# A decoder layer on one core: one seven-product k-pair less in the first key pair and one more in three up pairs, splits asked for earlier, and the last k-pair's order reversed

## The chip, the cores and the metric

The kernel runs on one core of a Trainium2 chip. The metric is the device time of one execution in microseconds, of which the median over several runs is taken. Three runs of the kernel before gave 1991.73 us as their median (1990.47 to 1993.38).

## The reference

One layer of a decoder on 256 tokens of width 2048, in float32: a retention mixer and a gated linear recurrence in parallel, merged by sigmoid gates; cross-attention to 256 memory tokens; a gated feed-forward part with a causal convolution; a final RMS norm.

```python
def memory_cross_attention(hn, mem_n, w_q, w_k, w_v, w_o):
    q = (hn @ w_q).reshape(b, s, XA_HEADS, XA_HEAD_DIM)
    k = (mem_n @ w_k).reshape(b, m, XA_HEADS, XA_HEAD_DIM)
    v = (mem_n @ w_v).reshape(b, m, XA_HEADS, XA_HEAD_DIM)
    logits = jnp.einsum("bshd,bmhd->bhsm", q, k).astype(jnp.float32) * (XA_HEAD_DIM ** -0.5)
    p = jax.nn.softmax(logits, axis=-1).astype(v.dtype)
    return jnp.einsum("bhsm,bmhd->bshd", p, v).reshape(b, s, D_MODEL) @ w_o

def conv_gated_ffn(hn, w_up, conv_w, conv_b, w_down):
    up = causal_dwconv(hn @ w_up, conv_w, conv_b)
    gate, val = jnp.split(up, 2, axis=-1)
    return (jax.nn.silu(gate) * val) @ w_down

# in the layer
hn = rmsnorm(h, norm_mix_w[l])
q, k, v, g_ret, xr, yr, g_a, g_b = jnp.split(hn @ w_in[l], offsets, axis=-1)
...
h = h + merged @ w_mix_out[l]
mem_n = rmsnorm(mem, norm_mem_w[l])
h = h + memory_cross_attention(rmsnorm(h, norm_xa_w[l]), mem_n, xa_w_q[l], xa_w_k[l], xa_w_v[l], xa_w_o[l])
h = h + conv_gated_ffn(rmsnorm(h, norm_ffn_w[l]), ffn_w_up[l], ffn_conv_w[l], ffn_conv_b[l], ffn_w_down[l])
return rmsnorm(h, final_norm_w)
```

The widths: 2048 for the model, 5632 for the feed-forward part, 4 attention heads of 512.

## The kernel before

**Products.** Every matmul takes a 128x128 block of tokens as the stationary operand and 128x512 weights as the moving one, in a reduced-precision float format. To keep float32 accuracy each operand is split in two, a high part (a cast, `hi` on ACT, L350) and a low part (the rest, `lo` on DVE, L351), and a product is three matmuls: high by high, low by high, high by low. The tokens' splits are called `s` (L613 and L614 for a load that is scaled on the way), the weights' ones `hi` and `lo`.

**Pairs and k-pairs.** Most weight matrices are worked through in *pairs*: two blocks of 512 columns at once, for both halves of the 256 tokens. The depth of 2048 is cut into 8 *k-pairs* of two 128-rows each; a k-pair's weights come as one 1 MB load (`raw`, three buffers). `steps_pair` (L476) runs one pair. A plain k-pair is 2 token halves x 2 column halves x 2 rows x 3 = 24 matmuls. Some k-pairs are done in *seven products* instead of eight, as in Strassen's scheme with sums of blocks on both sides: 7 x 3 = 21 matmuls. For that the weights' four sums are formed in place on DVE (L371) by `seven_parts`, which makes seven blocks and so 3 splits of 1024 columns and one of 512 where a plain k-pair has two of 1024; and the tokens' sums `ts` are formed by `sums_of` (L443: `g` L449, three `tq` L455 to L457, a high part on ACT L459, a low part on DVE L460). A token sum is kept and used again by later pairs on the same tokens. Which k-pairs are done so is a tuple in the plan: `SEVEN` = (2, 5), `SEVEN_O` = (3, 5), `SEVEN_U` = (4,), `SEVEN_V` = (5,).

**Accumulators.** `p2` and `p4` (left column block, two token halves) lie in one of three slots of the `acc` pool, `x3` and `n` (right column block) are the two buffers of the `sm` pool, which attention's and retention's small products use too. The seven's other four (`p1`, `p6`, `p7`, `x5`) take two more `acc` slots and are drained after the last seven (L515 to L522) into `o1` and `o2`, the left and the right block. At the pair's end four adds (L532) bring `p2`, `p4`, `x3` and `n` in.

**Order.** TensorE's matmuls run in program order. The other engines' instructions are put in order at build time by a list scheduler that works by priorities; `tc.high_priority` moves some ahead. The weights' splits are asked for two loads ahead (`AHEAD`, L391). `later(n, fn)` puts work n + 1 chunks of weights behind. SP issues all loads and the DMA transposes, in one order. A block of results is turned from rows to columns by `by_dma` (L546): copies to planes on ACT (L554), two DMA transposes (L555), a copy back on ACT (L567, `f`), and then what uses it.

**Around the key pair.** `Pairs` (L663) holds a list of token splits that are made when they are asked for: `ms[k]` loads the memory's columns (`in_mem_t`) and splits them. The first four are asked for during the mixer's last product (L1056), the others by `t = st[k2]` in `steps_pair`, at the k-pair itself. Sums are asked for up to three k-pairs ahead, but for lists only where the element is there already (L496). The order of products is: mixer output, key pair 0, query pair 0, query pair 2, attention of heads 0 and 1, key pair 2, value pair, attention of heads 2 and 3, two value blocks, output.

**Feed-forward part.** 11 up pairs (a gate block and its value block) in parts of 4, 4 and 3. The down product of a part, two pairs over the part's hidden values, stands behind the first up pair of the next; the last down product is done in single blocks. Each up pair's blocks are turned; the convolution (L1166, L1168: `fg`, `fv`) and the gating (L1178, L1179, L591) run during the next product.

Of the kernel before, what the change touches and what calls it, by code (L numbers as in the profile page):

```python
# [26 lines left out]
FF = 5632  # L27
NF = FF // P
BW = 512
KC = 4  # L30
KH = 2
# [10 lines left out]
SEVEN = (2, 5)  # L42
SEVEN_O = (3, 5)
SEVEN_U = (4,)
SEVEN_V = (5,)

O_Q, O_K, O_V, O_G = 0, 1024, 2048, 4096
# [22 lines left out]
def both(w, c, seven=SEVEN, row=0, nk=NT, apart=BW):  # L70

    return w, row, nk, (c, c + apart, seven)


def weight_plan():

    plan = []
    for g in range(2):
        keys = [("w_in", 0, NT, c + g * BW) for c in (O_Q, O_K)]
        values = [("w_in", 0, NT, O_V + b * BW) for b in range(2)]  # L80
        plan += keys + [both("w_in", O_V + 1024, SEVEN_V)] if g else [keys[0], values[0], keys[1], values[1]]
        plan.append(both("w_in", O_G + g * 1024))
    for b in range(4):
        plan += [("w_in", 0, NT, c + b * BW) for c in (O_XR, O_YR)]
    plan += [("w_in", 0, NT, O_GB + b * BW) for b in range(2)] + [both("w_proj_rnn", 0)]
    plan += [both("w_in", O_GB + 1024), both("w_proj_rnn", 1024)]
    plan += [both(w, c + b * BW) for w, c in (("w_in", O_GA), ("w_proj_ret", 0)) for b in (0, 2)]
    plan += [("w_mix_out", 0, NT, b * BW) for b in range(4)]
    plan += [both(w, b * BW) for w, b in (("xa_w_k", 0), ("xa_w_q", 0), ("xa_w_q", 2), ("xa_w_k", 2))]
    plan += [both("xa_w_v", 0)] + [("xa_w_v", 0, NT, b * BW) for b in (2, 3)]  # L90
    plan += [both("xa_w_o", 0, SEVEN_O)] + [("xa_w_o", 0, NT, b * BW) for b in (2, 3)]
    for kind, *a in ff_plan():
        if kind == "down" and sum(a) < NF // 4:
            plan += [both("ffn_w_down", b * BW, SEVEN, a[0] * BW, 4 * a[1]) for b in (0, 2)]
        elif kind == "down":
            plan += [("ffn_w_down", a[0] * BW, 4 * a[1], b * BW) for b in range(4)]
        else:
            plan.append(both("ffn_w_up", a[0] * BW, SEVEN_U, apart=FF))
    return plan


def gate_up_at():

    return [w for w, *_ in weight_plan()].index("ffn_w_up")


def ff_plan():

    out, b0 = [], 0
    for nb_ in FF_PARTS:  # L110
        ups = [("up", b) for b in range(b0, b0 + nb_)]
        if b0:
            ups[1:1] = [("down",) + before]
        out += ups
        before = (b0, nb_)
        b0 += nb_
    return out + [("down",) + before]
# [48 lines left out]
def hybrid_layer(  # L166
# [34 lines left out]
    def big(shape, dt=F32, s="b"):  # L201
        return bp.tile(shape, dt, tag="big", name=nm(s))

    def tmp(s="t"):
        return tp.tile([P, 2, S], F32, tag="tmp", name=nm(s))

    def acc():
        return pm.tile([P, 2, BW], F32, tag="acc", name=nm("acc"))

    def small(shape=(P, 2, S)):  # L210
        return px.tile(list(shape), F32, tag="sm", name=nm("sm"))
# [39 lines left out]
    def mm(*a, **k):  # L251
        tc.keep_in_program_order(pe.matmul(*a, **k))  # L252


    plan = weight_plan()
    stream = weight_stream()
    ahead, taken, gemms = [], [0], [0]
# [180 lines left out]
    def gemm_n(*args):  # L438
        return ended(steps_n(*args))
# [3 lines left out]
    def sums_of(t, src=None, scale=None):  # L443

        if id(t) in token_sums:
            return token_sums[id(t)][1]
        if src is None:
            src = big([P, 2, S], s="g")
            dve.tensor_tensor(  # L449
                out=src, in0=t[:, :, 0:S].bitcast(F32), in1=t[:, :, S:BW].bitcast(F32), op=ALU.add  # L450
            )
        o = big([P, 2, 4, P], F32R, s="ts")
        s = tmp("tq").rearrange("p a (b n) -> p (a b) n", b=2)
        a = src.rearrange("p j (i n) -> p (j i) n", i=2)
        dve.tensor_tensor(out=s[:, 0:2], in0=a[:, 0:2], in1=a[:, 1::2], op=ALU.subtract)  # L455
        dve.tensor_tensor(out=s[:, 2], in0=s[:, 1], in1=a[:, 0], op=ALU.subtract)
        dve.tensor_tensor(out=s[:, 3], in0=a[:, 2], in1=s[:, 2], op=ALU.add)  # L457
        if scale is None:
            act.copy(o[:, 0], s)  # L459
            dve.tensor_tensor(out=o[:, 1], in0=s, in1=o[:, 0].bitcast(F32), op=ALU.subtract)  # L460
        else:
            act.mul(o[:, 0], s, scale)
            dve.scalar_tensor_tensor(
                out=o[:, 1], in0=s, scalar=scale, in1=o[:, 0].bitcast(F32), op0=ALU.mult, op1=ALU.subtract
            )
        token_sums[id(t)] = (t, o)
        return o
# [8 lines left out]
    def steps_pair(w, row, st, nk, c1, c2):  # L476

        seven = plan[gemms[0]][3][2]
        last = max(seven)
        banks, begun = {}, set()  # L480
        banks["p2"], banks["p4"] = (lambda a: (a[:, 0, :], a[:, 1, :]))(acc())
        banks["x3"], banks["n"] = (small((P, BW)) for _ in range(2))

        def rows_of(name, left, right, end):

            o = banks[name]
            for i, (a, b) in enumerate(((0, 0), (1, 0), (0, 1))):
                mm(o, left[a], right[b], start=name not in begun, stop=end and i == 2, skip_group_check=True)
                begun.add(name)

        o1 = o2 = None
        for k0, n, parts in chunks(nk, w, row, (c1, c2, seven)):
            k2 = k0 // KH
            for i in seven:
                if k2 < i <= k2 + 3 and (not isinstance(st, list) or i < len(st)):
                    sums_of(st[i])  # L496
            t = st[k2]
            own = [
                [(t[:, j, i * P : (i + 1) * P], t[:, j, S + i * P : S + (i + 1) * P]) for j in range(2)]
                for i in range(2)  # L500
            ]
            if k2 in seven:
                if "p1" not in banks:
                    for a, b in (("p1", "p6"), ("p7", "x5")):
                        two = acc()
                        banks[a], banks[b] = two[:, 0, :], two[:, 1, :]
                ts = sums_of(t)
                s3, s1, s2, s4 = ((ts[:, 0, i, :], ts[:, 1, i, :]) for i in range(4))
                lefts = (own[0][0], s4, own[0][1], s1, s3, s2, own[1][1])
                for name, l, r in zip(("p1", "x3", "p2", "x5", "p7", "p6", "p4"), lefts, parts):  # L510
                    rows_of(name, l, r, k2 == last and name in ("p1", "x5", "p7", "p6"))
                if k2 == last:
                    o1, o2 = (big([P, 2, BW], s="o") for _ in range(2))
                    with tc.high_priority(FREE):
                        act.copy(o1[:, 0, :], banks["p1"])  # L515
                        for o, a, b, op in (
                            (o2[:, 0, :], o1[:, 0, :], banks["p6"], ALU.add),
                            (o1[:, 1, :], o2[:, 0, :], banks["p7"], ALU.add),
                            (o2[:, 1, :], banks["x5"], o1[:, 1, :], ALU.subtract),
                            (o2[:, 0, :], banks["x5"], o2[:, 0, :], ALU.subtract),  # L520
                        ):
                            dve.tensor_tensor(out=o, in0=a, in1=b, op=op)  # L522
            else:
                end = k0 + n == nk
                for b, names in enumerate((("p2", "p4"), ("x3", "n"))):
                    for tt, name in enumerate(names):
                        for j in range(KH):
                            rows_of(name, own[tt][j], parts[b * KH + j], end and j == KH - 1)
            yield o1, o2
        with tc.high_priority(FREE):  # L530
            for o, a in ((o1[:, 0, :], "p2"), (o1[:, 1, :], "p4"), (o2[:, 0, :], "x3"), (o2[:, 1, :], "n")):
                dve.tensor_tensor(out=o, in0=o, in1=banks[a], op=ALU.add)  # L532

    def pair(*args):
        return ended(steps_pair(*args))
# [279 lines left out]
    for g in range(2):  # L815
        dec = big([P, 4, S], s="dec")
        vs, turned = [], ([], [])
        for b, o in enumerate((O_Q, O_K)):
# [5 lines left out]
            a = gemm_n("w_in", 0, xs, NT, o + g * BW) if g + b else q0  # L824
# [516 lines left out]
```

## Time and profile before

| | us |
|---|---|
| median of three runs | 1991.73 (1990.47 to 1993.38) |
| profiled execution | 1992.14 |
| its span, first to last instruction | 1990.0 |
| ACT busy | 1392.4 (70%) |
| DMA queues' busy share, mean of 16 engines | 64.3% |

The profile comes from one execution. The page lists, for each engine, its busy time and its count of instructions; groups of instructions carry the line of the program that made them, here often a helper's (L252 for every matmul). A wait such as `PE sm L252 <- DVE o L532` reads: TensorE's matmul into `sm` stood still until DVE's instruction of L532 was done; behind it stand the total time, the number of waits and the longest. In a timeline a row has its start, its duration, the instruction, how often it ran in a row, and in brackets the idle time of the engine before it and what ended it. Matmuls overlap, so a single one shows 0.39 us though the next one starts earlier than that.

### The profile page before, as it was taken

How to read it: one execution, taken by the hardware profiler on the slowest of the kernel's cores; microseconds unless marked ns; L12 is line 12 of the kernel's file. 1: busy time of each engine (PE TensorE's matmuls, PEld its weight loads, DVE VectorE, ACT ScalarE, POOL GpSimd, SP SyncE). 2: the span in 40 equal slices, each digit the busy share in tenths (PEclk: the TensorE clock that was granted, in tenths of full speed). 3: DMA queues.
4: the chain of work that ended last, by engine and by line, in shares of the span. 5: the costliest groups of instructions: out<-in, count | busy, mean ns of one | idle time of the engine just before them, and what ended most of it. 6: DMA issues, size and time to landing. Idle time of an engine off the chain costs nothing.

```text
span 1990.0 us, 24148 instructions
## 1 busy us (share of the span) xinstructions
PE 1966.6 (99%) x8804; PEld 1628.2 (82%) x8804; DVE 1632.3 (82%) x2164; ACT 1392.4 (70%) x1710; POOL 26.1 (1%) x25
## 2 busy tenths in 40 slices
PE   9999999999999999998999999999999999999998
PEld 8888788888888888886888888888888888888887
DVE  6887986899898888767988767778889878899686
ACT  7666658989654656595868677778776577774683
POOL 0000011000000000000000000000000000000000
PEclk9999999999999999998999999999999999999999
DMA  8756567665554556996666666666666567666673
GB/s 332 236 212 181 198 231 204 201 221 192 214 209 169 210 193 200 318 294 201 217 206 201 214 219 221 204 216 218 220 214 211 212 198 224 212 212 234 209 243 117
DMA packets 198343, 429.82 MB, mean 216 GB/s; under 512 B 142160, under 2 KB 146768, under 8 KB 153168
## 3 DMA queue, kind: packets, MB, share of 16 engines
q1 hardware_dynamic: 198224, 428.28, 64.3%
q8 instruction: 69, 1.13, 0.2%
q14 instruction: 50, 0.41, 0.1%
HBM read 390.49 MB, written 4.19 MB: 198 GB/s over the span
## 4 chain that ended last, share of the span: by engine, by line
PE 37%; DVE 8%; ACT 4%; DMA 2%; issue 2%; POOL 0%; POOLq 0%; DVEq 0%; ACTq 0%; SPq 0%
PE acc L252 23%; PE sm L252 14%; DVE lo L351 3%; ACT hi L350 1%; DMA raw<-in_wall 1%; DMA pt<-pl 1%; ACT f L567 1%; ACT pl L554 1%; DVE fg L1168 1%; DVE raw L371 1%; DVE fv L1168 1%; DVE o L522 1%; ACT o L1282 0%; DVE s L591 0%; DVE fo L1179 0%
## 5 line engine op out<-in xcount | busy, mean ns | idle before, releaser
L351 DVE TENSOR_TENSOR lo<-raw,hi 128x1024 fp32r<-128x1024 f32 (+1 forms) x814 | 951.3, 1195 | 275.2 <-ACT hi L350 270.3
L252 PE MATMUL acc<-hi,s 128*128 128x512 f32 (+1 forms) x3636 | 1116.8, 389 | 3.9 <-DVE s L614 2.2
L350 ACT CAST hi<-raw 128x1024 fp32r<-128x1024 f32 (+1 forms) x814 | 804.8, 1021 | 410.2 <-PE acc L252 109.2
L252 PEld LDWEIGHTS acc<-hi,s 128*128 128x128 f32 x3636 | 680.8, 188 | 145.0 <-DVE s L614 4.3
L252 PE MATMUL acc<-lo,s 128*128 128x512 f32 (+1 forms) x1818 | 705.8, 388 | 2.0 <-DVE lo L351 1.9
L252 PE MATMUL sm<-hi,s 128*128 128x512 f32 x1584 | 488.7, 390 | 1.9 <-DVE o L532 1.9
L252 PEld LDWEIGHTS acc<-lo,s 128*128 128x128 f32 x1818 | 341.9, 188 | 73.4 <-DVE lo L351 3.2
L252 PEld LDWEIGHTS sm<-hi,s 128*128 128x128 f32 x1584 | 297.8, 188 | 64.7 <-ACT v L602 2.0
L252 PE MATMUL sm<-lo,s 128*128 128x512 f32 x792 | 308.5, 390 | 0.0
L567 ACT COPY f<-pt 128x1024 uint16<-128x1024 uint16 x128 | 166.8, 1354 | 15.2 <-DMA pt<-pl 14.9
L252 PEld LDWEIGHTS sm<-lo,s 128*128 128x128 f32 x792 | 148.9, 188 | 31.0
L371 DVE TENSOR_TENSOR raw<-raw 128x512 f32<-128x512 f32 x200 | 138.1, 691 | 3.1
L252 PE MATMUL acc<-hi,ts 128*128 128x512 f32 x300 | 92.9, 391 | 0.0
L554 ACT COPY pl<-o 128x1024 uint16<-128x1024 uint16 x68 | 67.6, 1040 | 6.7 <-DVE o L1002 6.7
L252 PEld LDWEIGHTS acc<-hi,ts 128*128 128x128 f32 x300 | 56.6, 189 | 11.9
L252 PE MATMUL acc<-lo,ts 128*128 128x512 f32 x150 | 59.0, 393 | 0.9 <-DVE lo L351 0.8
L554 ACT COPY pl<-rows 128x1024 uint16<-128x1024 uint16 x40 | 39.8, 1044 | 20.6 <-DVE rows L578 10.6
L532 DVE TENSOR_TENSOR o<-o,acc 128x512 f32<-128x512 f32 x62 | 39.9, 689 | 7.3 <-PE acc L252 7.3
L522 DVE TENSOR_TENSOR o<-o,acc 128x512 f32<-128x512 f32 x62 | 42.6, 687 | 0.1
L532 DVE TENSOR_TENSOR o<-o,sm 128x512 f32<-128x512 f32 x62 | 40.9, 689 | 0.1
L522 DVE TENSOR_TENSOR o<-acc,o 128x512 f32<-128x512 f32 x62 | 40.0, 690 | 0.4
L1168 DVE SCALAR_TENSOR_TENSOR fv<-f,pf,fv 128x255 f32<-128x255 f32 (+1 forms) x88 | 38.7, 486 | 0.0
(191 smaller groups left out, 1054.9 us busy)
## 6 DMA issues: line engine op xcount, KB each, us to landing
raw<-in_wall SPq DMA_DIRECT2D x352, 1024.0 KB, 4.8
nat<-in_x SPq DMA_DIRECT2D x8, 512.0 KB, 9.3
raw<-in_wall SPq DMA_DIRECT2D x7, 512.0 KB, 5.8
pt<-pl SPq DMA_TRANSPOSE x128, 3.3
nat<-in_mem SPq DMA_DIRECT2D x4, 512.0 KB, 9.1
home<-nat SPq DMA_DIRECT2D x4, 512.0 KB, 6.6
nat<-home SPq DMA_DIRECT2D x4, 512.0 KB, 7.2
xt<-in_x_t SPq DMA_DIRECT2D x3, 512.0 KB, 9.1
```

What stands on the lines that cost most here:

```text
L252: tc.keep_in_program_order(pe.matmul(*a, **k))
L350: act.copy(hi[:, cs], src[:, cs])
L351: dve.tensor_tensor(out=lo[:, cs], in0=src[:, cs], in1=hi[:, cs].bitcast(F32), op=ALU.subtract)
L371: dve.tensor_tensor(out=o, in0=a, in1=b, op=ALU.add)
L522: dve.tensor_tensor(out=o, in0=a, in1=b, op=op)
L532: dve.tensor_tensor(out=o, in0=o, in1=banks[a], op=ALU.add)
L554: act.copy(planes[:, tt], words[:, tt])
L567: act.copy(halves_[:, :, :, cs], turned_[:, :, :, cs])
L1168: dve.scalar_tensor_tensor(out=y[:, s:S], in0=z[:, j, 0 : S - s], scalar=pf[:, 2 - s, t : t + 1], in1=y[:, s:S], op0=ALU.mult, op1=ALU.add,)
```

## The change

Four edits.

- The first key pair (`xa_w_k`, block 0) is planned with `SEVEN_V` in place of `SEVEN`: k-pair 5 in seven products and no longer k-pair 2. In the same line the blocks' columns are written as 2 * BW; the pairs are the same.
- In `steps_pair`, where the tokens are a `Pairs`, the splits of two k-pairs ahead are asked for, behind the test for the sums and ahead of `t = st[k2]`.
- An up pair gets `MORE_U` = (2, 4) in place of `SEVEN_U` = (4,) where the plan's entry ahead of it is not an up pair. These are the first up pair of the first part and the second of the other two, because in these the down product stands between the first and the second.
- In the last k-pair of each pair the right block (`x3`, `n`, with the second half of the weights) comes ahead of the left one (`p2`, `p4`), and the four adds at the end follow this order.

```diff
+MORE_U = (2, 4)
...
-    plan += [both(w, b * BW) for w, b in (("xa_w_k", 0), ("xa_w_q", 0), ("xa_w_q", 2), ("xa_w_k", 2))]
+    plan += [both("xa_w_k", 0, SEVEN_V), both("xa_w_q", 0), both("xa_w_q", 2 * BW), both("xa_w_k", 2 * BW)]
...
-            plan.append(both("ffn_w_up", a[0] * BW, SEVEN_U, apart=FF))
+            plan.append(both("ffn_w_up", a[0] * BW, MORE_U if plan[-1][0] != "ffn_w_up" else SEVEN_U, apart=FF))
...
             for i in seven:
                 if k2 < i <= k2 + 3 and (not isinstance(st, list) or i < len(st)):
                     sums_of(st[i])
+            if isinstance(st, Pairs):
+                st[min(nk // KH - 1, k2 + 2)]
             t = st[k2]
...
                 end = k0 + n == nk
-                for b, names in enumerate((("p2", "p4"), ("x3", "n"))):
+                blocks = list(enumerate((("p2", "p4"), ("x3", "n"))))
+                for b, names in reversed(blocks) if end else blocks:
                     for tt, name in enumerate(names):
...
         with tc.high_priority(FREE):
-            for o, a in ((o1[:, 0, :], "p2"), (o1[:, 1, :], "p4"), (o2[:, 0, :], "x3"), (o2[:, 1, :], "n")):
+            for o, a in ((o2[:, 0, :], "x3"), (o2[:, 1, :], "n"), (o1[:, 0, :], "p2"), (o1[:, 1, :], "p4")):
                 dve.tensor_tensor(out=o, in0=o, in1=banks[a], op=ALU.add)
```

## The prediction

> **What bounds the kernel now.** I read the page's first part, then the waits of TensorE, then the same stretch for each pair of column blocks, and last the timelines around the few places where TensorE stands still.
>
> ```profile
> span 1990.0 us, 24148 instructions
> PE 1966.6 (99%) x8804; PEld 1628.2 (82%) x8804; DVE 1632.3 (82%) x2164; ACT 1392.4 (70%) x1710; POOL 26.1 (1%) x25
> ```
>
> TensorE is busy 99% of the span. So only two things can move the end: fewer matmuls, or fewer of the 1990.0 - 1966.6 = 23.4 us in which it idles (and of the time in which it is busy at a slow clock). The waits say where those are:
>
> ```profile
> PE sm L252 <- ACT ts L459: 3.8, 2, 3.2
> PE sm L252 <- DVE o L532: 3.2, 4, 1.7
> PE acc L252 <- DVE lo L351: 2.7, 4, 1.0
> PE acc L252 <- DVE s L614: 2.2, 2, 1.7
> PE acc L252 <- ACT s L613: 1.4, 1, 1.4
> ```
>
> The change touches the first two, the fourth and the fifth. Next, stretches from the first matmul of one pair to the first of the next: the first key pair, the query pair behind it, two up pairs that the change extends, one late up pair, and the two down pairs that follow an up pair.
>
> ```profile
> 893.11:950.66 57.55, 49.12 (x187) 37.55 (x186) 44.11 (x64) 33.79 (x47) 0.72 (x1) 0.91 0.61 192
> 950.66:992.83 42.17, 42.17 (x188) 34.91 (x187) 38.97 (x51) 33.94 (x39) 0.00 (x0) 1.00 0.66 225
> 1273.41:1316.25 42.84, 42.84 (x190) 35.47 (x189) 33.26 (x42) 27.85 (x35) 0.70 (x1) 1.00 0.66 223
> 1573.96:1616.80 42.84, 42.84 (x191) 35.47 (x189) 31.27 (x34) 20.50 (x22) 0.00 (x0) 1.00 0.59 209
> 1488.46:1531.80 43.34, 42.50 (x188) 34.83 (x186) 40.43 (x59) 36.35 (x45) 0.00 (x0) 1.00 0.69 213
> 1745.56:1789.06 43.50, 42.45 (x187) 34.84 (x186) 40.29 (x59) 36.51 (x45) 0.00 (x0) 1.00 0.72 212
> ```
>
> Columns: stretch, its length, busy time of PE, PEld, DVE, ACT, POOL, granted clock, DMA share, GB/s. The key pair and the query pair have the same products: six k-pairs of 24 matmuls and two of 21, 186 in all. The query pair does them without a gap: 42.17 / 186 = 0.2267 us for one. The key pair needs 57.55, so 15.4 us are lost in this one place, at a granted clock of 0.91. Its timeline shows them:
>
> ```profile
> 905.42 0.50 PE L252 MATMUL sm<-hi,ts 128*128 128x512 f32 x1 [0.60 <-ACT ts L459]
> 906.51 0.50 PE L252 MATMUL sm<-hi,ts 128*128 128x512 f32 x1 [0.59 <-DVE ts L460]
> ...
> 926.24 0.51 PE L252 MATMUL sm<-hi,ts 128*128 128x512 f32 x1 [3.25 <-ACT ts L459]
> ...
> 927.98 1.05 PE L252 MATMUL acc<-hi,s 128*128 128x512 f32 x2
> ...
> 931.74 0.62 PE L252 MATMUL acc<-hi,s 128*128 128x512 f32 x2
> ...
> 934.00 0.51 PE L252 MATMUL acc<-hi,s 128*128 128x512 f32 x1 [1.41 <-ACT s L613]
> 936.15 0.50 PE L252 MATMUL acc<-hi,s 128*128 128x512 f32 x1 [1.65 <-DVE s L614]
> ...
> 937.74 0.80 PE L252 MATMUL acc<-hi,s 128*128 128x512 f32 x1 [0.58 <-DVE s L614]
> ...
> 938.76 1.05 PE L252 MATMUL acc<-hi,s 128*128 128x512 f32 x2
> ...
> 943.46 0.54 PE L252 MATMUL sm<-lo,s 128*128 128x512 f32 x1
> ```
>
> In brackets stands the idle time and what ended it. Token sums (ts) of k-pairs 2 and 5 come late, then the splits (s) of k-pair 6. Behind the long wait and behind the last ones two matmuls take 1.05 where at 931.74 they take 0.62: the clock is halved, the second time from about 938.3 to 943.5, which costs half of these 5.2 us, 2.6.
>
> **The change part by part.** *First key pair, one seven instead of two.* K-pair 2 becomes plain: +3 matmuls, 3 x 0.2267 = +0.68 us. Its token sums, four weight sums and two of its splits disappear (6 us of DVE work, at the prices below), and the waits at 905.42 and 906.51 with them, for plain products need no ts.
>
> *Splits two k-pairs ahead.* The splits of k-pairs 4 to 7 are asked at 2 to 5, so those of 6 and 7 now stand in front of the weight splits of their own k-pairs; the waits at 934.00, 936.15 and 937.74 go. The sums of k-pair 5 are asked one k-pair earlier than before, no more: the test on the list's length stands ahead of the line that lengthens it. Can they still be late? These rows price the chain:
>
> ```profile
> 905.28 1.34 ACT L567 COPY f<-pt 128x1024 uint16<-128x1024 uint16 x1
> 909.58 1.72 ACT L613 ACTIVATE s<-f,pb 128x256 fp32r<-128x256 f32 x4
> 915.32 0.69 DVE L371 TENSOR_TENSOR raw<-raw 128x512 f32<-128x512 f32 x1
> 920.44 2.37 DVE L351 TENSOR_TENSOR lo<-raw,hi 128x1024 fp32r<-128x1024 f32 x2
> 923.44 0.42 DVE L455 TENSOR_TENSOR tq<-g 128x256 f32<-128x256 f32 x1
> 925.24 0.29 DVE L457 TENSOR_TENSOR tq<-g,tq 128x128 f32<-128x128 f32 x1
> ```
>
> Rows overlap by some 0.1 us, so I use 1.25 for f, 0.6 for 512 elements, 0.4 for 256, 1.14 for a low part, 0.95 for a high part (estimates from these rows and the spacing of their neighbours). In the changed order ACT does, from 905.28: two f, one high part, four s, one high part, two s, one high part: 2.5 + 0.95 + 1.6 + 0.95 + 0.8 + 0.95 = 7.8, to 913.1. DVE then does: low part, s, weight sum, half low part, weight sum, s, weight sum, g, weight sum, low part, three tq, low part, ts: 1.14 + 0.4 + 0.6 + 0.6 + 0.6 + 0.4 + 0.6 + 0.6 + 0.6 + 1.14 + 0.9 + 1.14 + 0.6 = 9.3, to 922.4. TensorE reaches k-pair 5 at 893.11 + 120 x 0.2267 = 920.3 and wants the low ts after four matmuls, at 921.2. So 1.2 us are missing if f starts as it did; it started then behind a ts that is gone, and could start up to 1.6 us earlier, with which nothing is missing. Between 0 and 1.2 I take 0.7. [...] The pair: 42.17 + 0.68 + 0.7 = 43.55, which is **-14.0 us**. On the DMA queue the memory load of k-pairs 4 and 5 moves ahead of one weight load; one issue takes 0.43 us (next row), and the weight load it delays is wanted two k-pairs, 10.9 us, later: nothing.
>
> ```profile
> 909.18 0.43 SPq L223 DMA_DIRECT2D xt<-in_mem_t  x1
> ```
>
> [...]
>
> *A second seven in the first up pair of each part.* "First" is the one whose forerunner in the plan is not an up pair: the 1st, 6th and 10th, for in the later parts the down product stands behind one up pair. 3 x 3 matmuls less: 9 x 0.2267 = **-2.04 us**. Each adds on DVE four weight sums (0.6), one low part of 1024 (1.14) and one of 512 (0.6): 4.1 us; the first also builds the sums of k-pair 2 (g, three tq, ts: 0.6 + 0.9 + 0.6 = 2.1). DVE then has 33.26 + 6.2 = 39.5 of 42.2 in the first, 31.27 + 4.1 = 35.4 in the sixth. ACT's extra 1.5 to 2.1 us find 27.85 and 20.50 busy. Room in both; in the first it is thin, 0 to +1 us. I take 0.
>
> *Last k-pair reversed.* The two `sm` accumulators (x3, n) end 12 matmuls, 2.7 us, earlier and are added first; `acc` (p2, p4) ends last. What waited for the drained `sm` banks:
>
> ```profile
> 233.50 0.70 PE L252 MATMUL sm<-hi,s 128*128 128x512 f32 x2 [1.66 <-DVE o L532]
> 1035.54 0.63 PE L252 MATMUL sm<-s,s 128*128 128x256 f32 x3 [0.39 <-DVE o L532]
> 1126.86 0.86 PE L252 MATMUL sm<-s,s 128*128 128x256 f32 x5 [0.96 <-DVE o L532]
> ```
>
> These and a fourth of 0.2 are the 3.2 us of the waits' second row, and I take **-3.2 us**. `acc` has three slots and the next pair wants the late one only at its first seven, over 10 us later: nothing. The price is elsewhere. The last k-pair now begins with the right half of its weights, whose split is made second. Where DVE is behind, it is not there yet. The first matmul of the last k-pair in the down pair of either part, and the split of its right half:
>
> ```profile
> 1526.36 0.62 PE L252 MATMUL acc<-hi,s 128*128 128x512 f32 x2
> ...
> 1783.62 0.62 PE L252 MATMUL acc<-hi,s 128*128 128x512 f32 x2
> ```
>
> ```profile
> 1526.92 1.24 DVE L351 TENSOR_TENSOR lo<-raw,hi 128x1024 fp32r<-128x1024 f32 x1
> ...
> 1784.23 1.23 DVE L351 TENSOR_TENSOR lo<-raw,hi 128x1024 fp32r<-128x1024 f32 x1
> ```
>
> The low part is first read by the third matmul, 0.45 us in: at 1526.81 but ready at 1528.16, and at 1784.07 but ready at 1785.46. 1.35 and 1.39 us late, **+2.7 us**. Before, it was wanted 12 matmuls later and was in time. The lower end is 0, if DVE gains as much on the way (40.4 busy in 43.3 leaves 2.9). For the upper end, the up pair ahead of the down pair:
>
> ```profile
> 1483.02 0.61 PE L252 MATMUL acc<-hi,s 128*128 128x512 f32 x2
> ```
>
> ```profile
> 1482.81 1.24 DVE L351 TENSOR_TENSOR lo<-raw,hi 128x1024 fp32r<-128x1024 f32 x1
> ```
>
> Ready at 1484.05, wanted at 1483.47: 0.6 late, 1.2 in both parts, so 3.9 in all. In the changed order one add of 0.6 us stands behind this split and no longer ahead of it, so I count nothing here.
>
> The left block is now complete at the pair's end and not before: its turn by DMA, and so the gate convolution of each up pair, starts some 2 us later, and one weight load stands ahead of the transposes in the DMA queue (one issue, as above). That convolution waits for it on DVE, and with it the splits that are queued behind. A late up stage:
>
> ```profile
> 1445.00:1488.00 43.00, 42.64 (x187) 34.72 (x186) 37.15 (x53) 34.01 (x42) 0.00 (x0) 1.00 0.68 212
> ```
>
> With 37.15 of 43.0 busy DVE can hold 2 us; I take 0, and as the other end 0.5 for each of eight up pairs with a forerunner, 4 us (a quarter of the delay, an estimate).
>
> **Sum.** -14.0 - 2.04 - 3.2 + 2.7 = -16.5. The profiled execution took 1992.14 (its span of 1990.0 and 2.1 around it), 0.4 above the median of 1991.73. So 1975.6 beside the profile, 1975.2 beside the median; I say **1975.4**.
>
> **The rivals.** *The sums stay late* (15%): k-pair 5 still waits 3.25 and the clock halves as it did at 938, 2.6: 5.85 in place of 0.7, so 1980.6. For it: the sums are asked only one k-pair sooner and still stand behind four weight sums. Against: some 6 us of DVE work ahead of them are gone. [...]
>
> *Backlog in the feed-forward part* (13%): the later gate costs its 4, the thin first up pair its 1, the swap 3.9 in place of 2.7: 1981.6. For it: DVE is at 86 to 93% there, and waits for low parts exist already. Against: an up stage leaves 6 us.
>
> *The swap costs all over* (5%): slower. If in each of the 15 pairs from the first up pair on the right half were 1.6 us late at the last k-pair, that took 24 us against gains of 14.0 + 2.04 + 3.2 = 19.2: 1996.5. It decides from 19.2 / 15 = 1.3 us on average. Against: 1.4 are missing in two pairs only, and the query pair has DVE at 38.97 of 42.17 without a wait.
>
> *The split line does nothing* (4%): if the splits stayed where they were in the queues, 934 to 943 would keep 1.41 + 1.65 + 0.58 + 2.6 = 6.2: 1981.6. Against: in the changed order they stand ahead of the weight splits.
>
> **How the numbers follow.** That leaves the forecast 63%. Its own ends: no late sums and no late halves, 1975.4 - 0.7 - 2.7 = 1972.0; upward it meets the rivals. The range 1971.5 to 1981.5 holds the forecast, the sums that stay late and half of the other two faster cases: 63 + 15 + 8, less some for what I cannot see, 80%. Within 0.2%, 4 us, this kernel can't be told from no change. Faster 0.92, same 0.03, slower 0.05.
>
> **What would show it.** 8798 matmuls. From the first key matmul to the next pair's first 43 to 44 us at a granted clock near 1.0, with no wait for ts above 1.3 and none for s. No TensorE wait for the adds at a pair's end. New waits of `sm` matmuls for low parts at the end of the two down pairs, 1.4 each. The three longer up pairs at 42.2 each. A key pair above 47 us, or new waits for low parts above 6 us in all, would make the forecast wrong.

## The result, and the profile after

The changed kernel takes 1982.37 us (median of 5 runs, 1980.59 to 1983.18) where the kernel before, beside it, takes 1992.06: a ratio of 0.9951 (95% interval 0.9936 to 0.9965). It is faster by 9.7 us, not by the 16.5 of the forecast, and the time lies 0.9 above the top of the range. The profiled execution took 1982.85.

The page's first part, and the waits of TensorE (the line that was waited for, the sum, how many, the longest). Lines of the changed kernel stand 1 to 4 below those of before: L253 is the matmul, L351 and L352 the weights' high and low parts, L536 the adds at a pair's end.

```profile
span 1980.9 us, 24128 instructions
PE 1961.0 (99%) x8798; PEld 1624.5 (82%) x8798; DVE 1644.8 (83%) x2176; ACT 1394.1 (70%) x1714; POOL 31.6 (2%) x25
```

```profile
PE acc L253 <- DVE lo L352: 5.6, 7, 1.7
PE sm L253 <- DVE lo L352: 2.7, 3, 1.3
PE sm L253 <- DVE o L536: 0.9, 1, 0.9
PE acc L253 <- ACT hi L351: 0.8, 1, 0.8
```

There are 8798 matmuls, as forecast. The waits for token sums and token splits are gone, and of four waits for the adds one is left. In their place TensorE waits 8.3 us for low parts (2.7 before) and 0.8 for a high part.

The stretches, in the order of the program: the third of the mixer output's four stretches, the first key pair, the value pair with the two attention heads behind it, the first up pair, and the first down pairs of parts 1 and 2. Columns as in the prediction: stretch, length, busy times, clock.

```profile
826.81:872.28 45.47, 44.10 (x194) 35.88 (x192) 24.91 (x28) 34.55 (x45) 0.70 (x1) 1.00 0.95 330
894.04:936.88 42.84, 42.84 (x191) 35.48 (x189) 37.30 (x52) 30.45 (x44) 0.69 (x1) 1.00 0.78 267
...
1069.14:1118.22 49.08, 48.16 (x235) 40.59 (x234) 39.82 (x47) 35.36 (x41) 0.00 (x0) 1.00 0.67 220
1258.88:1301.04 42.16, 42.16 (x187) 34.92 (x186) 38.77 (x52) 29.42 (x38) 5.82 (x1) 1.00 0.63 224
1474.37:1520.73 46.36, 43.34 (x187) 34.53 (x186) 41.60 (x60) 36.54 (x46) 0.00 (x0) 1.00 0.62 203
...
1733.58:1779.78 46.20, 43.30 (x187) 34.53 (x186) 41.44 (x59) 36.37 (x46) 0.00 (x0) 1.00 0.62 204
```

The same stretches were 43.89, 57.55, 49.14, 42.84, 43.34 and 43.50. All stretches of the two profiled executions put together (a plus is a stretch that got longer):

| where | forecast, us | measured, us |
|---|---|---|
| first key pair | -14.0 | -14.7 |
| three up pairs with a second seven | -2.04 | -2.04 (three times 0.68) |
| waits for the adds behind three pairs | -3.2 | -3.1 (-2.42, -0.65, -0.06) |
| first down pair of parts 1 and 2 | +2.7 | +5.7 |
| second `w_proj_ret` pair and mixer output | 0 | +2.2 |
| up pairs 3 and 5 of the feed-forward part, and the 9th | 0 | +0.9 |
| start of the kernel, and what lies behind the last matmul | 0 | +1.8 |
| the rest | 0 | +0.1 |
| sum | -16.5 | -9.1 (1990.0 to 1980.9) |

The start and the tail are not touched by the change. They differ between executions: from the last matmul to the end of the span it is 7.2 us before, 8.1 here, and 7.2 to 8.9 in the experiments below. The rest of the gap is the reversal: it was to give 3.2 and cost 2.7, and it gave 3.1 and cost 8.8 (5.7 + 2.2 + 0.9).

Where TensorE stands still in the first down pair of part 1, from the timelines; the first row is the wait at the last k-pair but one, the second the one at the last.

```profile
1508.60 0.49 PE L253 MATMUL acc<-lo,s 128*128 128x512 f32 x1 [1.65 <-DVE lo L352]
...
1515.62 0.50 PE L253 MATMUL sm<-lo,s 128*128 128x512 f32 x1 [1.27 <-DVE lo L352]
```

The second is the forecast's 1.35, late right half. The first was 0.84 before, and 1.05 in part 2, and its growth was not in the sum:

```profile
1521.20 0.50 PE L252 MATMUL acc<-lo,s 128*128 128x512 f32 x1 [0.84 <-DVE lo L351]
```

What makes it is seen 20 us earlier. First DVE of the kernel before, then of the changed one, from the adds that end the up pair to the first row of the gate convolution (`fg`):

```profile
1488.54 1.30 DVE L532 TENSOR_TENSOR o<-o,acc 128x512 f32<-128x512 f32 x2
...
1496.94 0.69 DVE L351 TENSOR_TENSOR lo<-raw,hi 128x512 fp32r<-128x512 f32 x1 [1.45 <-ACT hi L350]
...
1500.06 2.36 DVE L351 TENSOR_TENSOR lo<-raw,hi 128x1024 fp32r<-128x1024 f32 x2 [0.56 <-ACT hi L350]
1503.17 1.23 DVE L351 TENSOR_TENSOR lo<-raw,hi 128x1024 fp32r<-128x1024 f32 x1 [0.76 <-ACT hi L350]
1504.32 3.24 DVE L1168 SCALAR_TENSOR_TENSOR fg<-f,pf,fg 128x255 f32<-128x255 f32 x8
```

```profile
1475.44 1.28 DVE L536 TENSOR_TENSOR o<-o,sm 128x512 f32<-128x512 f32 x2
...
1478.50 1.28 DVE L536 TENSOR_TENSOR o<-o,acc 128x512 f32<-128x512 f32 x2
...
1485.32 3.50 DVE L352 TENSOR_TENSOR lo<-raw,hi 128x1024 fp32r<-128x1024 f32 x3 [2.88 <-ACT hi L351]
1490.59 1.23 DVE L352 TENSOR_TENSOR lo<-raw,hi 128x1024 fp32r<-128x1024 f32 x1 [1.77 <-ACT hi L351]
1491.73 3.24 DVE L1172 SCALAR_TENSOR_TENSOR fg<-f,pf,fg 128x255 f32<-128x255 f32 x8
```

Counted from the down pair's first matmul (1488.46 before, 1474.37 after), the left block's adds start at 0.1 before and at 4.1 after, and the convolution at 15.9 and 17.4; the prediction had some 2 us for the turn and the convolution. In between DVE idles 1.45 + 0.56 + 0.76 = 2.8 before and 2.88 + 1.77 = 4.65 after, each time for ACT's high parts. From the convolution on DVE has no idle row in either kernel until the pair's end: what it lost ahead of that point it can't make up. Why ACT is late, from its timeline before and in the changed kernel:

```profile
1490.04 1.33 ACT L1282 ACTIVATE o<-o,ro 128x512 f32<-128x512 f32 x2
...
1493.16 1.34 ACT L1282 ACTIVATE o<-o,ro 128x512 f32<-128x512 f32 x2
```

```profile
1476.16 1.34 ACT L1286 ACTIVATE o<-o,ro 128x512 f32<-128x512 f32 x2 [0.93 <-DVE o L536]
...
1479.22 1.34 ACT L1286 ACTIVATE o<-o,ro 128x512 f32<-128x512 f32 x2 [1.21 <-DVE o L536]
1480.46 3.87 ACT L558 COPY pl<-o 128x1024 uint16<-128x1024 uint16 x4
1484.24 2.94 ACT L351 CAST hi<-raw 128x1024 fp32r<-128x1024 f32 x3
1487.09 2.56 ACT L571 COPY f<-pt 128x1024 uint16<-128x1024 uint16 x2
```

ACT works through these rows one after the other. The scaling of the two blocks (L1286) and the copies for the turn (L558) stand ahead of three high parts, and ACT now stands 0.93 + 1.21 = 2.1 us in front of the scalings, waiting for the adds; before, these scalings (L1282) have no wait in front of them. Counted as above, the copies back (`f`) end 1.5 later, and the convolution follows them.

At the mixer output the late left block is that of the second `w_proj_ret` pair, and what is late behind it is the DMA queue. SP's queue before, and after:

```profile
810.61 3.38 SPq L555 DMA_TRANSPOSE pt<-pl  x2
...
824.30 3.71 SPq L223 DMA_DIRECT2D raw<-in_wall  x3
```

```profile
812.50 2.61 SPq L559 DMA_TRANSPOSE pt<-pl  x2
...
825.65 3.31 SPq L224 DMA_DIRECT2D raw<-in_wall  x3
```

The mixer output begins at 805.70 and 805.05. So the turn starts 4.9 us into it before and 7.45 after, and the weight loads behind the transposes and the token loads at 18.6 and 20.6. These weights then come late: TensorE of the changed kernel at that point, in its first wait of two:

```profile
838.69 0.73 PE L253 MATMUL acc<-hi,s 128*128 128x512 f32 x2 [0.84 <-ACT hi L351]
```

### The profile page after: what moved, and what is told of

The parts are those of the page before. It is cut to its first block, busy times and chain, and to the rows that moved or that the text cites. A ratio compares the mean times of both kernels' runs of the same rounds, so it can differ in the third digit from the quotient of the medians.

```text
span 1980.9 us, 24128 instructions
## 1 busy us (share of the span) xinstructions
PE 1961.0 (99%) x8798; PEld 1624.5 (82%) x8798; DVE 1644.8 (83%) x2176; ACT 1394.1 (70%) x1714; POOL 31.6 (2%) x25
## 5 line engine op out<-in xcount | busy, mean ns | idle before, releaser
L352 DVE TENSOR_TENSOR lo<-raw,hi 128x1024 fp32r<-128x1024 f32 (+1 forms) x818 | 953.7, 1189 | 249.2 <-ACT hi L351 244.0
L253 PE MATMUL acc<-hi,s 128*128 128x512 f32 (+1 forms) x3632 | 1113.9, 388 | 0.9 <-ACT hi L351 0.8
L351 ACT CAST hi<-raw 128x1024 fp32r<-128x1024 f32 (+1 forms) x818 | 807.8, 1018 | 417.2 <-DMA raw<-in_wall 111.3
L253 PEld LDWEIGHTS acc<-hi,s 128*128 128x128 f32 x3632 | 679.3, 188 | 140.2 <-ACT hi L351 1.5
L253 PE MATMUL acc<-lo,s 128*128 128x512 f32 (+1 forms) x1816 | 704.5, 388 | 3.9 <-DVE lo L352 3.8
L253 PE MATMUL sm<-hi,s 128*128 128x512 f32 x1568 | 482.9, 389 | 0.0
L253 PEld LDWEIGHTS acc<-lo,s 128*128 128x128 f32 x1816 | 341.2, 188 | 76.3 <-DVE lo L352 6.5
L253 PEld LDWEIGHTS sm<-hi,s 128*128 128x128 f32 x1568 | 294.4, 188 | 61.1
L253 PE MATMUL sm<-lo,s 128*128 128x512 f32 x784 | 305.5, 390 | 2.8 <-DVE lo L352 2.7
L253 PEld LDWEIGHTS sm<-lo,s 128*128 128x128 f32 x784 | 147.2, 188 | 34.8 <-DVE lo L352 4.5
L372 DVE TENSOR_TENSOR raw<-raw 128x512 f32<-128x512 f32 x208 | 143.1, 688 | 3.7
L253 PE MATMUL acc<-hi,ts 128*128 128x512 f32 x312 | 96.2, 389 | 0.0
L558 ACT COPY pl<-o 128x1024 uint16<-128x1024 uint16 x68 | 66.7, 1039 | 7.9 <-DVE o L1006 5.2
L253 PEld LDWEIGHTS acc<-hi,ts 128*128 128x128 f32 x312 | 58.5, 188 | 12.2 <-ACT hi L351 0.2
L253 PE MATMUL acc<-lo,ts 128*128 128x512 f32 x156 | 61.5, 394 | 1.7 <-DVE lo L352 1.7
L558 ACT COPY pl<-rows 128x1024 uint16<-128x1024 uint16 x40 | 39.8, 1042 | 21.1 <-DVE rows L584 10.9
L536 DVE TENSOR_TENSOR o<-o,acc 128x512 f32<-128x512 f32 x62 | 39.6, 680 | 2.9 <-PE acc L253 2.7
L536 DVE TENSOR_TENSOR o<-o,sm 128x512 f32<-128x512 f32 x62 | 40.8, 680 | 0.3
```

Source lines behind the costliest of these rows:

```text
L351: act.copy(hi[:, cs], src[:, cs])
L352: dve.tensor_tensor(out=lo[:, cs], in0=src[:, cs], in1=hi[:, cs].bitcast(F32), op=ALU.subtract)
L372: dve.tensor_tensor(out=o, in0=a, in1=b, op=ALU.add)
L558: act.copy(planes[:, tt], words[:, tt])
```

## The experiments

The theory at this point: the reversal costs 8.8 us, by two ways. The right half of the weights is split second, and so late where DVE is behind; and the left block is turned later, which makes ACT, DVE and the DMA queue late. The rival: the second seven and its token sums, which are kept through the part, crowd DVE in the feed-forward part. Each run stands beside runs of the kernel before on the same chip, to which its ratio belongs. The intervals of e7, e8, e10, e11 and e12 overlap, so the differences of 1 to 4 us between these kernels can't be told from their times alone; they are read from the stretches of one profiled execution of each. A stretch that no edit reaches repeats well: the query pair behind the first key pair takes 42.16 in the profile of every kernel here.

| kernel | median, us | before, us | ratio (95% interval) |
|---|---|---|---|
| e1_no_reverse | 1978.16 | 1993.25 | 0.9925 (0.9911 to 0.9940) |
| e2_reverse_only | 2001.35 | 1993.25 | 1.0039 (1.0024 to 1.0054) |
| e3_right_split_first | 1981.21 | 1993.25 | 0.9940 (0.9925 to 0.9955) |
| e4_one_seven_u | 1986.46 | 1993.25 | 0.9961 (0.9947 to 0.9975) |
| e5_no_splits_ahead | 1985.17, one run | 1993.34 | |
| e6_key_two_sevens | 1988.14, one run | 1993.34 | |
| e7_three_pairs | 1971.37 | 1993.34 | 0.9894 (0.9878 to 0.9911) |
| e8_not_up_nor_ret | 1974.26 | 1993.34 | 0.9906 (0.9892 to 0.9921) |
| e9_adds_only | 1977.52 | 1991.58 | 0.9932 (0.9911 to 0.9953) |
| e10_and_ret | 1974.31 | 1991.58 | 0.9907 (0.9891 to 0.9924) |
| e11_and_down | 1975.76 | 1993.04 | 0.9912 (0.9898 to 0.9927) |
| e12_and_up | 1973.45 | 1993.04 | 0.9899 (0.9882 to 0.9915) |

**Without the reversal, and the reversal alone.** In the first the loop over the two blocks and the adds have their old order:

```diff
-                blocks = list(enumerate((("p2", "p4"), ("x3", "n"))))
-                for b, names in reversed(blocks) if end else blocks:
+                for b, names in enumerate((("p2", "p4"), ("x3", "n"))):
```

> The changed kernel with the last k-pair in its old order (left block first, and the adds too); the other three edits stay. Changed kernel: 1982.4 us. Theory (the reversal costs 8.8 us in new waits of TensorE and saves 3.1 at the pairs' ends): 1982.4 - 8.8 + 3.1 = 1976.7. The first down pair of parts 1 and 2 goes from 46.4 and 46.2 back to 43.3 and 43.5 us, the mixer output from 89.0 to 87.4, and the four waits for the adds return (3.2). Rival (the second seven and its kept token sums crowd DVE in the feed-forward part): the down pairs stay near 46, and only the 3.1 is lost: 1985.5.

The second is the kernel before with just these lines and the adds turned round.

> The kernel before with the reversed last k-pair alone. Kernel before: 1992.1 us. Theory: 1992.1 + 8.8 - 3.1 = 1997.8, with the first down pairs of parts 1 and 2 at 46 us and the mixer output at 89, so slower than before. Rival (the second seven crowds the feed-forward part): the reversal saves its 3.1 and costs nothing, 1989.0, down pairs at 43.4.

The first takes 1978.16 and the second 2001.35. The first down pairs without the reversal; then, with nothing but the reversal, the mixer output's third stretch (the down pair of part 1 takes 46.37 there):

```profile
1475.33:1518.61 43.28, 42.46 (x188) 34.83 (x186) 40.39 (x59) 36.38 (x45) 0.00 (x0) 1.00 0.69 215
1732.07:1775.69 43.62, 42.50 (x187) 34.84 (x186) 40.34 (x59) 36.47 (x45) 0.00 (x0) 1.00 0.72 212
```

```profile
826.26:873.56 47.30, 44.09 (x194) 35.88 (x192) 24.91 (x28) 34.65 (x44) 0.70 (x1) 1.00 0.92 322
```

The waits of the down pairs and of the mixer output come and go with the reversal, and the reversal by itself is a loss, of 8.1 us where 5.7 was expected: it loses 3.4 in the mixer output's third stretch (43.89 before), where the changed kernel loses 1.6, and 1.5 in the fifth up pair, where that loses 0.6. The kernel without it missed its 1976.7 by 1.5; one of the waits for the adds that came back, behind the value pair, is 2.0 long where it was 1.0 before, which accounts for 1.0 of it.

**The second seven.** Undone alone:

```diff
-            plan.append(both("ffn_w_up", a[0] * BW, MORE_U if plan[-1][0] != "ffn_w_up" else SEVEN_U, apart=FF))
+            plan.append(both("ffn_w_up", a[0] * BW, SEVEN_U, apart=FF))
```

> The changed kernel without the second seven in the three up pairs. Theory (the reversal alone makes the new waits): the three pairs go from 42.2 back to 42.8 us and nothing else moves, 1982.4 + 2.0 = 1984.4, with the first down pairs still at 46. Rival (the second seven and its kept token sums crowd DVE): the down pairs go back to 43.4, 1982.4 + 2.0 - 5.7 = 1978.7.

1986.46, and the first down pairs stay at 46.38 and 46.41. The rival falls. The time is 2.1 above the expected 1984.4; the five executions lie between 1983.2 and 1987.95.

**Is it the order of the splits?** The last k-pair's right half is split ahead of its left half, as the matmuls read them:

```diff
+                elif isinstance(c, tuple) and not (stream[taken[0]][0] == name and stream[taken[0]][1] > row):
+                    if k == 0:
+                        right = weight_parts(raw[:, KH:])
+                        parts = weight_parts(raw[:, one]) + right
                 else:
                     parts += weight_parts(raw[:, one])
```

> The changed kernel, but the weights of a pair's last k-pair are split in the order in which the matmuls now read them: the right half first. If the late right half of the weights is the reversal's price: the sm matmuls' waits for low parts at the last k-pair go (1.3 us in each of the two down pairs, 0.4 to 0.9 elsewhere, 3 in all), 1979.4; the waits at the last k-pair but one of the down pairs (1.8 each) stay, because the left block is still turned late. If only the late left block matters, these waits move elsewhere and the time stays within 1 us of 1982.4.

1981.21, 1.2 us less than with the change and 1.8 more than expected; the ratios, 0.9940 and 0.9951, lie within each other's interval, so the stretches have to tell. The waits at the last k-pair go in both down pairs, but not all that follows:

```profile
1475.35:1520.50 45.15, 43.05 (x187) 34.60 (x186) 40.38 (x59) 36.56 (x45) 0.00 (x0) 1.00 0.61 204
1733.34:1777.29 43.95, 42.49 (x187) 34.84 (x186) 39.19 (x58) 35.51 (x44) 0.00 (x0) 1.00 0.63 207
```

The first is 1.2 and the second 2.25 shorter than with the change. The wait at the last k-pair but one stays at 1.65 in the first, the mixer output's third stretch stays at 45.48, and two up pairs get 0.9 and 1.0 longer while a third gets 0.5 shorter. So the late right half is one part of the price (3.5 us in the down pairs, of which the up pairs take back 1.4) and not the larger one.

**Which pairs earn and which pay.** The remaining kernels reverse some pairs only: the matmul loop and the adds are turned round where a condition on the weights' name and column holds. First the three pairs behind which the adds were waited for:

```diff
+        turned = (w, c1) in (("w_in", O_V + 1024), ("xa_w_q", 1024), ("xa_w_v", 0))
...
-                for b, names in reversed(blocks) if end else blocks:
+                for b, names in reversed(blocks) if end and turned else blocks:
```

> The changed kernel with the reversed last k-pair only in the three pairs behind which the adds were waited for: the last retention values, the second query pair, the first cross-attention values. Theory (the reversal's price is paid in the feed-forward part and at the mixer's output, its gain is made behind these three pairs): against the kernel without any reversal (1978.2) the waits for the adds go, 2.3 + 0.65 + 1.1 = 4, and no wait for low parts is added: 1974.2. If the price is paid behind these pairs too: 1978 or more.

1971.37, 2.8 less than expected and 22 below the kernel before in the same runs; against the kernel without reversal the value pair alone gives 2.3 where 1.1 was expected. None of its waits is for the adds; the longest sum is for low parts:

```profile
PE acc L253 <- DVE lo L352: 2.1, 3, 0.9
```

The value pair with its heads takes 47.91, where the changed kernel takes 49.08. Its wait for the adds is gone altogether, while 0.9 of it stays in the changed kernel, which reverses the pairs ahead of it too.

Next, everything reversed but the up pairs and `w_proj_ret`, with the right half split first:

```diff
+        turned = w not in ("w_proj_ret", "ffn_w_up")
```

> The changed kernel with the right half of the last k-pair's weights split first, and with the old order in the pairs of ffn_w_up and w_proj_ret. The kernel with the right half first everywhere took 1981.2. Theory (what is left of the price comes from the left block of these pairs, which is turned later, so that what it feeds on DVE and in the DMA queue is late): the mixer output goes from 45.5 back to 43.8 in its third stretch, the up pairs to 42.8 and 43.7, the first down pairs from 45.2 and 44.0 to 43.4, though these keep the reversed order: 1981.2 - 6.9 = 1974.3. Rival (the reversed order of the down pairs themselves makes their waits): the down pairs stay at 45.2 and 44.0, 1976.5.

1974.26, as expected. The first down pairs keep their reversed order and take 43.36 and 43.51. So with the split order mended the rest of their loss came from the up pairs ahead of them. The mixer output's third stretch takes 44.25, not the 43.8 expected.

Then, on top of the three pairs, one family at a time: `w_proj_ret`, the down pairs, the up pairs.

```diff
+        turned = (w, c1) in (("w_in", O_V + 1024), ("xa_w_q", 1024), ("xa_w_v", 0)) or w == "w_proj_ret"
```

> The kernel that reverses three pairs only (1971.4), with the two pairs of w_proj_ret reversed as well. If the mixer output's loss comes from these pairs, whose left block then reaches its transposes and the weight loads behind them in the DMA queue later: the second of the pairs takes 42.7 in place of 42.2, the third stretch of the mixer output 45.4 in place of 43.5, and the kernel 1971.4 + 2.5 = 1973.9. If something else in the full reversal makes it: 1971.4.

> The kernel that reverses three pairs only (1971.4), with the down pairs reversed as well; the up pairs keep the old order. The prediction's own term for the reversal, taken by itself: in the first down pair of parts 1 and 2 the right half of the last k-pair's weights is 1.4 us late, 43.2 + 1.4 = 44.6 and 43.4 + 1.4 = 44.8, and nothing else moves: 1971.4 + 2.8 = 1974.2. If DVE's backlog there is made by the down pair's own reversed order, the wait at the k-pair before grows too, to 1.8: 1976.

> The kernel that reverses three pairs only (1971.4), with the up pairs reversed as well; the down pairs keep the old order. Theory (the up pair's left block comes later, ACT stands waiting for it ahead of the high parts, DVE loses 2 us there and has no room later in the down pair): the wait for low parts at the last k-pair but one of the down pairs grows from 0.85 and 1.1 to 1.8, up pairs 2 to 4 lose 0.5 to 1 each, and the first down pairs take 44.3 to 45: 1971.4 + 3.5 = 1974.9. If the up pairs can hold the 2 us, as the prediction took it: 1971.4.

`w_proj_ret`: 1974.31. The second of its pairs and the mixer output's third stretch:

```profile
761.56:804.29 42.73, 42.46 (x188) 34.84 (x187) 36.79 (x43) 30.06 (x34) 0.00 (x0) 1.00 0.61 194
826.05:871.90 45.85, 44.09 (x194) 35.88 (x192) 25.36 (x28) 34.99 (x45) 0.70 (x1) 1.00 0.97 330
```

That is 0.57 and 2.33 above the kernel with three pairs (42.16 and 43.52): the loss of 2.9 us in these two stretches is this family's. The medians differ by 2.9 too, the ratios by 0.0013, 2.6 us.

Down pairs: 1975.76. The waits at their last two k-pairs in part 1 (in part 2 they are 1.12 and 1.24):

```profile
1502.50 0.50 PE L253 MATMUL acc<-lo,s 128*128 128x512 f32 x1 [0.79 <-DVE lo L352]
1509.51 0.50 PE L253 MATMUL sm<-lo,s 128*128 128x512 f32 x1 [1.28 <-DVE lo L352]
```

Only the wait at the last k-pair is new. Measured from one matmul's start to the next, it costs 1.44 and 1.40 beyond the usual 0.23, the forecast's 1.35 and 1.39; the wait before it is near its old size (0.69 and 0.94 with three pairs). The two pairs, at 44.81 and 45.19, are 3.4 longer than with three pairs (43.18 and 43.43), where 2.8 was expected; by the ratios the kernels differ by 3.6, by the medians by 4.4.

Up pairs: the median is 1973.45, 2.1 above the kernel with three pairs (1.0 by the ratios), and the profiled execution is the slowest of four at 1978.98, the others taking 1972.5 to 1973.7. Its down pairs, and the wait at the last k-pair but one of part 1 (1.64 in part 2):

```profile
1474.27:1519.06 44.79, 43.04 (x187) 34.60 (x186) 40.03 (x59) 36.46 (x45) 0.00 (x0) 1.00 0.63 205
1731.90:1776.32 44.42, 42.78 (x187) 34.64 (x186) 39.68 (x58) 36.00 (x45) 0.00 (x0) 1.00 0.62 205
```

```profile
1508.51 0.50 PE L253 MATMUL acc<-lo,s 128*128 128x512 f32 x1 [1.66 <-DVE lo L352]
```

The down pairs have their old order here and still lose 1.6 and 1.0. DVE's idle times ahead of the convolution are those of the changed kernel to the digit, 2.88 and 1.77. Counted from the pair's first matmul the convolution starts 1.66 later than with three pairs in part 1 (17.36 and 15.70) and 1.01 later in part 2 (16.97 and 15.96): the down pairs lose what the convolution loses. This execution loses more in up pairs, 1.7 in the fifth and 3.7 in the third, of which the last section tells; the times of the other three leave no room for all of that.

**The order of the adds alone.** Matmuls in the old order, the four adds in the new one.

```diff
-                for b, names in reversed(blocks) if end else blocks:
+                for b, names in blocks:
```

> The changed kernel with the matmuls of the last k-pair in their old order (left block first); only the four adds are reversed, the right block's first. Beside it stands the kernel without any reversal (1978.2). Theory (a left block that is complete later makes work late on DVE and in the DMA queue, whatever makes it later): the left block is at most two adds, 1.2 us, later, about half of what the reversed matmuls do; the waits for the adds shrink from 4.2 to about 2, and half of the 4.7 in the feed-forward part and of the 2 around the mixer's output comes, 3.3: 1979.5. Rival (only the reversed matmuls cost): 1976.0, with the first down pairs at 43.4.

1977.52, between the two, and it tells less than meant. The scheduler put the adds behind the last `w_proj_ret` pair in the order left, left, right, right, and those behind the up pair ahead of the first down pair in the order left, right, left, right. The first transpose of the mixer output starts 4.89 us behind its first matmul, exactly as without any reversal, and the down pairs take 43.15 and 43.67. So the left block came hardly later, and next to nothing was lost; the waits for the adds stayed at 3.9. It neither supports nor refutes the theory.

**The key pair's two edits, one at a time**, on the kernel without reversal: without the line that asks for splits ahead, and with the old two sevens.

```diff
-            if isinstance(st, Pairs):
-                st[min(nk // KH - 1, k2 + 2)]
```

> The changed kernel with the old order of the last k-pair and without the line that asks for the splits two k-pairs ahead; the key pair keeps its one seven. Beside it stands the kernel with the line (1978.2, key pair 42.84 us). If the plan alone brings the sums of k-pair 5 forward and the line the splits of k-pair 6: the waits for s return (1.4 + 1.7 + 0.6, and 2.6 of halved clock), the waits for ts don't, the key pair takes 49 us and the kernel 1984.5. If the line also carries the sums, the wait of 3.3 for ts comes back as well, with its own halved clock: 55 us, 1990. If the line does nothing: 1978.2.

```diff
-    plan += [both("xa_w_k", 0, SEVEN_V), both("xa_w_q", 0), both("xa_w_q", 2 * BW), both("xa_w_k", 2 * BW)]
+    plan += [both("xa_w_k", 0), both("xa_w_q", 0), both("xa_w_q", 2 * BW), both("xa_w_k", 2 * BW)]
```

> The changed kernel with the old order of the last k-pair, and the first key pair in two sevens as before; the splits are asked for two k-pairs ahead. Beside it stands the kernel with one seven (1978.2, key pair 42.84 us). If the plan is what takes the late sums away: the waits for ts at k-pairs 2 and 5 stay (0.6 + 0.6 and 3.3, with 1.3 of halved clock), those for s go, the pair takes 42.2 + 6 = 48 us and the kernel 1983.5. If the line alone is enough, the pair takes 42.2 and the kernel 1977.5.

The key pair takes 50.82 and 52.40, where both edits together take 42.84. First the kernel without the line, then the one with two sevens:

```profile
928.59 0.49 PE L253 MATMUL acc<-hi,s 128*128 128x512 f32 x1 [2.96 <-ACT s L614]
930.74 0.80 PE L253 MATMUL acc<-hi,s 128*128 128x512 f32 x1 [1.66 <-DVE s L615]
```

```profile
929.18 1.52 PE L253 MATMUL sm<-hi,ts 128*128 128x512 f32 x2 [3.89 <-ACT ts L460]
...
930.93 1.05 PE L253 MATMUL acc<-hi,s 128*128 128x512 f32 x2
```

Without the line the splits of k-pair 6 are late and the sums are not; with two sevens the sums are late and the splits are not. So the plan brings the sums in time and the line the splits, as the prediction had it. Either alone leaves 8 to 10 us of the 15, because the wait that is left grows (2.96 where it was 1.41, and 3.89 where it was 3.25) and slow matmuls follow it (the granted clock of the pair is 0.93 in both). In the second kernel they go on to 935.5 (rows of 1.05 for two), which costs 3.2 us beyond the usual 0.227 for each, where 1.3 was counted; its waits come to 6.3, where 4.5 was counted. The second expectation was 4.4 too low mostly for these two.

## Why the prediction was wrong

- **The first key pair** was right in place and size: -14.7 against -14.0. The 0.7 for late sums was not needed. Nothing was counted for a slower clock in the changed pair, and its granted clock is 1.00. In the changed kernel's timeline the low part of the sums is done at 920.19 + 0.68 = 920.9, that is 26.8 after the pair's first matmul; the estimate from the prices of rows was 922.4 - 893.1 = 29.3, and TensorE wants it at about 28. The rivals of late sums and of a line that does nothing fall.
- **Nine matmuls less**: right, 0.68 in each of three pairs; the thin first up pair had no wait with DVE at 38.77 of 42.16.
- **The waits for the adds**: right in the sum (3.1), and this by luck. The first of the three pairs gave 2.42 and not the 1.66 + 0.2 of its waits' rows, the second 0.65 and not 0.39; the third, the value pair, gave 0.06 and not 0.96, because its wait is still there.
- **The late right half at the last k-pair** (+2.7): right for what it named. Reversing the down pairs alone makes new waits of 1.44 and 1.40 there.
- **The step that failed** is "With 37.15 of 43.0 busy DVE can hold 2 us; I take 0" for the left block that is turned later. The room is there in that up stage, but all of it lies ahead of the convolution, as idle time in which DVE waits for ACT (2.17 + 0.67 + 3.01 = 5.85 us):

```profile
1453.47 1.23 DVE L351 TENSOR_TENSOR lo<-raw,hi 128x1024 fp32r<-128x1024 f32 x1 [2.17 <-ACT hi L350]
1455.37 1.23 DVE L351 TENSOR_TENSOR lo<-raw,hi 128x1024 fp32r<-128x1024 f32 x1 [0.67 <-ACT hi L350]
1459.60 1.23 DVE L351 TENSOR_TENSOR lo<-raw,hi 128x1024 fp32r<-128x1024 f32 x1 [3.01 <-ACT hi L350]
1460.74 3.24 DVE L1168 SCALAR_TENSOR_TENSOR fg<-f,pf,fg 128x255 f32<-128x255 f32 x8
```

And most of the price was paid in another stage, the first down pairs of parts 1 and 2, which stand behind an up pair and whose room this step did not count. There DVE idles 2.8 us, again all ahead of the convolution, and TensorE already waited 0.84 and 1.05 for a low part. With the up pairs alone reversed the convolution starts 1.66 and 1.01 later and these pairs take 1.6 and 1.0 more: the delay goes through to TensorE. In the up pairs themselves it mostly does not: in the fifth one of the changed kernel the convolution starts 1.9 later and the pair is 0.6 longer. The other end that was given, 4 us, is near the 3.8 measured (2.9 of the down pairs' 5.7, and 0.9), but it was meant for eight up pairs, so this is luck.

- **The mixer output** was not in the sum at all. The prediction looked at the DMA queue only at the key pair and at an up pair, and counted one issue of 0.43 each time. It is not the issue that counts but that the transposes wait for the late block: the turn starts 2.5 later, the weight loads behind it 2.0, and reversing `w_proj_ret` alone costs 2.3 there and 0.6 in the second of its own pairs.
- **The rival that came nearest** is the backlog in the feed-forward part, at 1981.6. Of its terms the later gate came (3.8 for 4), the thin first up pair (1) and the larger swap (3.9 for 2.7) did not; the mixer output's 2.2 and the 1.8 by which start and tail happened to differ stand in their place. The range was too short above it, as the mixer output's loss was in no case.

Left open: why the value pair's wait grows from 1.0 to 2.0 without the reversal and stays at 0.9 where all pairs are reversed, why the up pairs take up a delay that the down pairs pass on, and what makes the start and the tail differ by up to 1.8 us between executions.

The version that reverses three pairs only beats both kernels, at 0.9894 of the kernel before (0.9878 to 0.9911), where the whole change has 0.9951 (0.9936 to 0.9965).

## What to carry to other kernels

An order that frees one buffer earlier makes another result later (here the left block's adds, by 4.0 us): apply it only to the pairs behind which somebody waits for that buffer, and look at what hangs on the result that comes later, in the stages behind it too. The average busy share of an engine was no measure here of the delay it could take; ask where in the stage its idle time lies, ahead of the point at which the delay enters or behind it, and whether somebody waits for it there already. And on ACT and in SP's queue, whose rows here ran one after the other, a late operand held up what stood behind it (the copies back by 1.5 us, the weight loads by 2.0), so it is the waiting time that is to be priced and not the issue.

## What was not expected of the hardware

One wait of 1.82 us was followed by slow matmuls in the profiled execution of the kernel with reversed up pairs, and the granted clock of that pair is 0.96:

```profile
1379.66 0.50 PE L253 MATMUL sm<-lo,s 128*128 128x512 f32 x1 [1.82 <-DVE lo L352]
...
1381.14 1.05 PE L253 MATMUL sm<-hi,s 128*128 128x512 f32 x2
```

From about 1380 to 1383.3 two matmuls take up to 1.05 in place of 0.62, though no other wait is near. The wait of 1.8 and the slow matmuls behind it cost 3.7 together, and that pair, the third up pair, took 46.56 in place of 42.84. In the kernel before, rows of 1.05 for two stand where the granted clock is 0.50, from 938.30 to 943.50; the longest wait in the 5 us ahead of that is 1.65. Waits of 2.04 and 2.28 behind the value pair in other kernels of this study (e1 and e5) were not followed by it: the matmuls behind them run at 0.13 each (29 in 3.73 us, 18 in 2.41), as behind the wait of 0.96 there in the kernel before (48 in 6.02). So the length of one wait did not decide it in these runs.
